# A Trainium2 decoder trunk: the front of the first feed-forward reordered, and more pairs of gate and up combined

## The chip, the cores and the metric

One core of a Trainium2 chip. The metric is the device time of one execution in microseconds; lower is better. A matrix product runs on TensorE (PE), elementwise work on VectorE (DVE), casts and activations on ScalarE (ACT), a few sums on GpSimd (POOL), and SyncE (SP) issues the transfers from main memory.

## The reference, cut to what matters

Two layers. Each has a feed-forward at half step, a mixing block (windowed attention beside gated linear attention), and a second feed-forward, so there are four feed-forwards, f = 0 to 3, on 512 tokens of width 1024:

```python
def rmsnorm(x, g):
    y = x * rsqrt(mean(x * x, axis=-1) + EPS)
    return y * g

def swiglu(h, w_gate, w_up, w_down):
    return (silu(h @ w_gate) * (h @ w_up)) @ w_down

h = rmsnorm(x, ffn1_norm[l])
x = x + 0.5 * swiglu(h, ffn1_w_gate[l], ffn1_w_up[l], ffn1_w_down[l])
```

w_gate and w_up are 1024 x 2816, w_down is 2816 x 1024. All inputs are float32.

## The kernel before, in words

x lies transposed: eight tiles x[d] of 128 features by 512 tokens. To keep float32 accuracy every operand of a large product is split into a rounded high half (a cast on ScalarE, line 112) and the rest (a subtraction on DVE, line 113), and each product is three matmuls, high by high, high by low, low by high (`mul3`, lines 182 to 184). Weights come as raw tiles of 1 MB in two buffers, issued on SP; their halves go into six rotating buffers each of `whi` and `wlo`, 512 columns apiece.

The 2816 hidden features are 22 blocks of 128, taken in two halves h of 11. For one block the columns of gate and up are worked on together, as a pair (the loop over j in `ffn`). After 11 pairs the products with w_down follow (eight outputs d, `Weights(wd[f, h, d], ...)`), which are added to x.

A pair is done in one of two ways. `plain(j)`: eight steps k, and in each three matmuls for gate and three for up, 128 x 128 by 128 x 512, so 48 matmuls of 512 columns. `combined(j)`: a scheme that makes the 2 x 2 blocks of weights and tokens out of seven products instead of eight; each product runs over four pairs of steps with three matmuls of 256 columns, 84 in all. It needs seven pieces of weights instead of four, four sums of raw weights on DVE (lines 166 to 173, class `Combined`), and sums of the outputs (lines 363 to 387). Its last two products are put off into the next pair (`rest`, `left`). The tuple `PLAIN` (line 48) names the pairs that are plain, counted over both halves: the first five, and 8, 11, 15 and 19.

The norm of a feed-forward is not ready when its first pair starts. The first three pairs of h = 0 run on x times the gain alone (`Norm.scaled`, lines 218 and 219: operands `uh`, `ul`), and their outputs are multiplied by the norm's factor afterwards (lines 342 and 343, in `gated`). The factor comes in steps. `squares` squares x[d] on ScalarE and sums on POOL (lines 260 to 264); in the first feed-forward the squares of d = 5 to 7 are kept apart (`direct`, line 256) and summed by PE. `scale` sums over features with matmuls of one column (line 275) and takes the power on POOL (line 280); `spread` brings the factor to all partitions with matmuls by the identity (line 286) and a copy on ScalarE (`rb`, line 289). `whole(d)` then makes the normalised x and splits it again into the same `uh`, `ul` (line 227 and `split`), for the pairs from j = 3 on; `combine(n)` makes the token sums that combined pairs need (lines 236 to 239 and two splits). In the code `scale` stands in pair 1 at step 2 and `spread` there at step 6, `whole(k)` in pair 2, `combine` in pairs 3 and 4.

The order of work: the program is written out by hand, a scheduler then sorts each engine's instructions by a priority that follows the order in the code; `tc.high_priority(offset)` moves a block ahead by so much, `PREP` = 400 for weights and `FIRST` = 5000 for the first pair's weights with the loads of x and their splits. Buffers of a name (`temp(2)` has four, PSUM pools `mm` and `sm` four each) make later users wait. Each engine runs its instructions strictly in the sorted order.

At the very start (lines 820 to 831): the load of the small vectors, the first pair's weights mixed with the loads of x, the constants `cst` (identity, ones, masks of attention, cosines, sines), the masks `mi` with a cast on DVE, and the squares.

Of the kernel before, what the change touches and what calls it, by code (L numbers as in the profile page):

```python
# [17 lines left out]
P = 128  # L18
# [3 lines left out]
KD = D // P  # L22
FF = 2816
NF = FF // P
NH = NF // 2
# [9 lines left out]
FIRST = 5000  # L35


C_ID, C_TRI, C_ONE, C_BO, C_AM, C_COS, C_SIN = 0, 128, 256, 257, 289, 545, 1057
# [6 lines left out]

H = T // 2

PLAIN = (0, 1, 2, 3, 4, 8, 11, 15, 19)

VB = 144  # L50
VCUT = (0, 400, 784, 1168)
# [3 lines left out]
def trunk(ctx, tc, xT, wgu, wd, wqk, wv, wg, wpa, wpb, wo, glaw, vecs, consts, masks, out):  # L55
    nc = tc.nc
    V, S, G, PE = nc.vector, nc.scalar, nc.gpsimd, nc.tensor
# [11 lines left out]
    def slot(tag, shape=(P, T), dtype=F32, bufs=1):  # L69
        big = int(np.prod(shape[1:])) >= 256  # L70
        return (pool if big else tiny).tile(list(shape), dtype, name=tag, tag=tag, bufs=bufs)

    def temp(n, shape=(P, T)):
        return slot(f"t{n}", shape, bufs=4)
# [4 lines left out]
    def psum():  # L79
        return sm.tile([P, T], F32, name="sm", tag="sm")  # L80

    def acc():
        return mm.tile([P, T], F32, name="mm", tag="mm")
# [7 lines left out]
    cst = cpool.tile([P, NCONST], F32, name="cst")  # L91
# [19 lines left out]
    def split(hi, lo, src):  # L111
        S.copy(hi, src)  # L112
        V.tensor_sub(lo, src, hi.bitcast(F32))  # L113
# [66 lines left out]
    def mul3(ps, w, a, start, stop, onto=False):  # L180

        PE.matmul(ps, w[0], a[0], start=start, stop=False, skip_group_check=onto)  # L182
        PE.matmul(ps, w[0], a[1], start=False, stop=False, skip_group_check=onto)  # L183
        PE.matmul(ps, w[1], a[0], start=False, stop=stop, skip_group_check=onto)  # L184
# [107 lines left out]
    def ffn(f, norm, nxt, spill, last):  # L292
        for h in range(2):
            g = []

            rest = []
            room = {}

            def left(n=2):
                while n and rest:  # L300
                    rest.pop(0)()
                    n -= 1

            def part(tag, n):

                if tag not in room:
                    room[tag] = slot(tag, (P, 2, T), F32R)
                return room[tag][:, n, :]

            def keep(j, tu):  # L310
                if j < 8:
                    hi, lo = slot(f"{'qk'[j % 2]}{j // 2}", dtype=F32R), part(f"v{j // 2}", j % 2)
                else:
                    hi, lo = (part(f"{sets[1]}{2 * z + (j - 8) // 2}", j % 2) for z in range(2))
                split(hi, lo, tu)
                g.append((hi, lo))

            def silu(to, z):
                tables[0] = S.activation(to, z, AF.Silu)

            def plain(j):
                raw = h == 0 and j < 3
                w = first if f + h + j == 0 else Weights(wgu[f, h * NH + j], KD, 256)
                pg, pu = acc(), acc()
                for k in range(KD):
                    if h == 0 and j == 1 and k == 2:
                        norm.scale()
                    if h == 0 and j == 1 and k == 6:
                        norm.spread()
                    if k in (2, 5):  # L330
                        left(1)
                    mul3(pg, w.at(k, 0, P), norm.u[k], k == 0, k == KD - 1)
                    mul3(pu, w.at(k, P, P), norm.u[k], k == 0, k == KD - 1)
                    if h == 0 and j == 2:
                        norm.whole(k)
                    if h == 0 and j in (3, 4) and k in (3, 7):
                        norm.combine(2 * j - 6 + k // 4)

                def gated():
                    tg, tu = temp(1), temp(2)  # L340
                    if raw:
                        V.tensor_mul(tg, pg, norm.rb)
                        V.tensor_mul(tu, pu, norm.rb)
                        silu(tg, tg)
                        V.tensor_mul(tu, tu, tg)
                    else:
                        silu(tg, pg)
                        V.tensor_mul(tu, pu, tg)
                    keep(j, tu)

                return gated

            def combined(j):
                w = Combined(wgu[f, h * NH + j])

                def run(to, n, start=False):
                    for k in range(4):
                        mul3(to, w.at(n, k), norm.c[k][n], start and k == 0, k == 3, not start)

                a = acc()[:, :H]  # L360
                run(a, 1, True)
                s12 = temp(1)
                S.copy(s12[:, :H], a)
                left(1)
                b = acc()[:, :H]
                run(b, 5, True)
                left(1)
                run(a, 6)
                S.copy(s12[:, H:], a)
                c = psum()[:, :H]  # L370
                run(c, 2, True)
                tg, su = temp(1), temp(2)
                V.tensor_add(tg[:, :H], c, s12[:, :H])
                run(a, 7)
                S.copy(su[:, :H], a)
                V.tensor_add(su[:, H:], b, su[:, :H])

                def up():
                    run(a, 4)

                def gate():
                    run(b, 3)
                    V.tensor_add(tg[:, H:], b, s12[:, H:])
                    silu(tg, tg)
                    tu = temp(2)
                    V.tensor_mul(tu[:, :H], a, tg[:, :H])
                    V.tensor_mul(tu[:, H:], su[:, H:], tg[:, H:])
                    keep(j, tu)

                rest.extend((up, gate))  # L390

            late = None
            for j in range(NH):
                if h * NH + j in PLAIN:
                    gated = plain(j)
                    if h == 0 and j == 0:
                        late = gated
                    else:
                        if late is not None:
                            late()  # L400
                            late = None
                        gated()
                else:
                    combined(j)
            left()
            for d in range(KD):
                w = Weights(wd[f, h, d], NH, P)
                ps = acc()
                for k in range(NH):
                    mul3(ps, w.at(k, 0, P), g[k], k == 0, k == NH - 1)  # L410
                V.scalar_tensor_tensor(x[d], ps, 0.5, x[d], op0=ALU.mult, op1=ALU.add)
                if h == 1:
                    if nxt is not None:
                        nxt.add(d)
                    if spill or last:
                        nc.sync.dma_start((xs if spill else out)[:, d, :], x[d])
# [400 lines left out]
    norm = Norm(0, V_F1)  # L817
# [3 lines left out]

    with tc.high_priority(offset=FIRST):
        nc.scalar.dma_start(vec, vecs)
    first = Weights(wgu[0, 0], KD, 256, 2, FIRST, (load, norm.scaled))
    mi = slot("v0", (P, 576), I32)
    with tc.high_priority(offset=PREP):
        nc.sync.dma_start(cst, consts)
        nc.sync.dma_start(mi, masks)
    for d in range(KD):
        norm.squares(d, d > 4)  # L830
    V.tensor_copy(msk, mi)

    ones = temp(1)
# [4 lines left out]
    for l in range(L):  # L838
        n2 = Norm(l, V_MIX)
        ffn(2 * l, norm, n2, True, False)  # L840
        g = temp(1)[0:96]
        nc.scalar.dma_start(g, glaw[:, l, :])
        n3 = Norm(l, V_F2)
        mix(l, n2, n3, g)
        norm = Norm(l + 1, V_F1) if l + 1 < L else None
        ffn(2 * l + 1, n3, norm, False, l + 1 == L)
# [117 lines left out]
```

## Time and profile before

| | us |
|---|---|
| median of three runs | 2351.91 (2349.49 to 2353.78) |
| the profiled execution | 2350.56 |
| its span on the core | 2348.8 |
| TensorE busy | 2323.8 (99%) |
| VectorE busy | 1520.7 (65%) |
| ScalarE busy | 1114.4 (47%) |
| POOL busy | 154.1 (7%) |

The page's busy times are averages over stages that differ; where work follows work its rows have a start and a duration. Operations of one engine overlap in part, so the distance from start to start says what one costs in a row, and the duration says when its result is there. A group of rows shows an idle time with its releaser in square brackets.

### The profile page before, as it was taken

How to read it: one execution, taken by the hardware profiler on the slowest of the kernel's cores; microseconds unless marked ns; L12 is line 12 of the kernel's file. 1: busy time of each engine (PE TensorE's matmuls, PEld its weight loads, DVE VectorE, ACT ScalarE, POOL GpSimd, SP SyncE). 2: the span in 40 equal slices, each digit the busy share in tenths (PEclk: the TensorE clock that was granted, in tenths of full speed). 3: DMA queues.
4: the chain of work that ended last, by engine and by line, in shares of the span. 5: the costliest groups of instructions: out<-in, count | busy, mean ns of one | idle time of the engine just before them, and what ended most of it. 6: DMA issues, size and time to landing. Idle time of an engine off the chain costs nothing.

```text
span 2348.8 us, 33948 instructions
## 1 busy us (share of the span) xinstructions
PE 2323.8 (99%) x12904; PEld 2011.7 (86%) x12904; DVE 1520.7 (65%) x2769; ACT 1114.4 (47%) x2077; POOL 154.1 (7%) x147
## 2 busy tenths in 40 slices
PE   8999999999999999999999999999999999999999
PEld 7889988787888889899889899887878888898997
DVE  7846755659755678467468467456596556773772
ACT  5534544554455345245445345454545644552551
POOL 1000010003110100000100000100131101000000
PEclk9999999999999999999999999999999999999999
DMA  5232234121123322322322322431112233223232
GB/s 179 75 111 97 101 122 135 64 81 37 55 90 117 117 90 85 122 91 96 111 90 85 122 90 87 144 123 64 68 37 72 90 125 109 90 92 115 90 100 90
DMA packets 73587, 226.68 MB, mean 97 GB/s; under 512 B 8720, under 2 KB 16912, under 8 KB 73424
## 3 DMA queue, kind: packets, MB, share of 16 engines
q1 hardware_dynamic: 71136, 221.46, 27.6%
q10 hardware_dynamic: 2288, 3.06, 0.5%
q8 instruction: 101, 1.65, 0.3%
q14 instruction: 62, 0.51, 0.1%
HBM read 215.58 MB, written 6.29 MB: 94 GB/s over the span
## 4 chain that ended last, share of the span: by engine, by line
PE 90%; DVE 7%; ACT 2%; issue 1%; POOL 0%; DMA 0%; SPq 0%; DVEq 0%; POOLq 0%; ACTq 0%
PE mm L182 26%; PE mm L184 26%; PE mm L183 25%; PE sm L674 2%; DVE wlo L113 1%; PE mm L518 1%; PE mm L520 1%; PE mm L519 1%; PE sm L183 1%; PE sm L182 1%; PE sm L184 1%; PE sm L580 1%; PE sm L611 1%; PE sm L605 1%; DVE t L658 0%
## 5 line engine op out<-in xcount | busy, mean ns | idle before, releaser
L112 ACT CAST whi<-raw 128x512 fp32r<-128x512 f32 (+2 forms) x976 | 588.9, 608 | 917.8 <-PE mm L183 798.6
L113 DVE TENSOR_TENSOR wlo<-raw,whi 128x512 fp32r<-128x512 f32 (+2 forms) x976 | 669.3, 690 | 491.5 <-ACT whi L112 480.3
L182 PE MATMUL mm<-uh,whi 128*128 128x512 f32 (+1 forms) x1584 | 579.7, 366 | 6.5 <-ACT uh L218 5.7
L183 PE MATMUL mm<-ul,whi 128*128 128x512 f32 (+1 forms) x1584 | 577.6, 365 | 0.0
L184 PE MATMUL mm<-uh,wlo 128*128 128x512 f32 (+1 forms) x1584 | 575.6, 364 | 1.0 <-DVE wlo L113 0.9
L182 PEld LDWEIGHTS mm<-uh,whi 128*128 128x128 f32 x1584 | 300.3, 190 | 52.0 <-ACT uh L218 5.7
L184 PEld LDWEIGHTS mm<-uh,wlo 128*128 128x128 f32 x1584 | 299.9, 189 | 49.0 <-DVE wlo L113 4.0
L183 PEld LDWEIGHTS mm<-ul,whi 128*128 128x128 f32 x1584 | 300.5, 190 | 44.7 <-DVE ul L219 0.5
L183 PE MATMUL mm<-v,whi 128*128 128x512 f32 x640 | 249.1, 389 | 0.0
L183 PEld LDWEIGHTS mm<-v,whi 128*128 128x128 f32 x640 | 120.2, 188 | 24.3
L182 PE MATMUL mm<-k,whi 128*128 128x512 f32 x320 | 124.6, 389 | 0.0
L182 PE MATMUL mm<-q,whi 128*128 128x512 f32 x320 | 124.5, 389 | 0.0
L184 PE MATMUL mm<-k,wlo 128*128 128x512 f32 x320 | 124.5, 389 | 0.0
L184 PE MATMUL mm<-q,wlo 128*128 128x512 f32 x320 | 124.5, 389 | 0.0
L264 POOL TENSOR_TENSOR sum<-sum,t 128x512 f32<-128x512 f32 x39 | 53.5, 1372 | 681.0 <-ACT t L263 385.3
L182 PE MATMUL mm<-b,whi 128*128 128x256 f32 (+1 forms) x272 | 85.9, 317 | 0.1
L184 PE MATMUL mm<-qr,wlo 128*128 128x256 f32 (+1 forms) x272 | 83.7, 308 | 0.0
L182 PE MATMUL mm<-qr,whi 128*128 128x256 f32 (+1 forms) x272 | 83.7, 308 | 0.0
L184 PE MATMUL mm<-b,wlo 128*128 128x256 f32 (+1 forms) x272 | 83.7, 308 | 0.0
L183 PE MATMUL mm<-o,whi 128*128 128x512 f32 x192 | 75.2, 392 | 0.0
L183 PE MATMUL mm<-x,whi 128*128 128x512 f32 x192 | 75.2, 392 | 0.0
L182 PEld LDWEIGHTS mm<-k,whi 128*128 128x128 f32 x320 | 60.1, 188 | 12.6
(326 smaller groups left out, 4218.6 us busy)
## 6 DMA issues: line engine op xcount, KB each, us to landing
raw<-in_wgu SPq DMA_DIRECT2D x174, 512.0 KB, 4.1
raw<-in_wd SPq DMA_DIRECT2D x64, 512.0 KB, 3.6
raw<-in_wg SPq DMA_DIRECT2D x48, 512.0 KB, 4.4
raw<-in_wqk SPq DMA_DIRECT2D x26, 512.0 KB, 4.4
raw<-in_wd SPq DMA_DIRECT2D x64, 192.0 KB, 3.7
raw<-in_wpb SPq DMA_DIRECT2D x16, 512.0 KB, 4.2
raw<-in_wo SPq DMA_DIRECT2D x16, 512.0 KB, 5.8
raw<-in_wv SPq DMA_DIRECT2D x16, 384.0 KB, 3.3
```

Source lines behind the costliest of these rows:

```text
L112: S.copy(hi, src)
L113: V.tensor_sub(lo, src, hi.bitcast(F32))
L182: PE.matmul(ps, w[0], a[0], start=start, stop=False, skip_group_check=onto)
L183: PE.matmul(ps, w[0], a[1], start=False, stop=False, skip_group_check=onto)
L184: PE.matmul(ps, w[1], a[0], start=False, stop=stop, skip_group_check=onto)
L264: G.tensor_tensor(self.sum, self.sum, sq, op=ALU.add)
L518: PE.matmul(ps, u[k][0][:, t], wh, start=k == 0, stop=False)
L519: PE.matmul(ps, u[k][0][:, t], wl, start=False, stop=False)
L520: PE.matmul(ps, u[k][1][:, t], wh, start=False, stop=k == KD - 1)
L580: PE.matmul(ps[half][:, j, k0:], stacked[2 * jp + j][:, half, t], z[:, half, n * P - P + k0:(n + 1) * P], start=z is kh, stop=z is kl)
L605: row = after(PE.transpose(pt[:, kc, j, :], s[half][:, j, kc * P:(kc + 1) * P], ident), row)
L674: PE.matmul(ps[:, i, :], ke[:, i, :], qe[:, i * 64:(i + 1) * 64], start=True, stop=True)
```

## The change

PLAIN keeps the first five pairs; 8, 11, 15 and 19 are combined. In the first feed-forward pair 5 is plain as well. There the second pair's weights get a higher priority, the sums of squares all go over POOL, `scale`, `spread`, `whole` and `combine` come later in the code, the gating of pairs 0 and 1 is put off until the factor is spread, pair 2 takes its accumulators from the other PSUM pool, five matmuls on zeros are put at the very start, and the constants are loaded in two parts, of which only the first keeps a priority, with the masks behind the second.

```diff
-PLAIN = (0, 1, 2, 3, 4, 8, 11, 15, 19)
+PLAIN = (0, 1, 2, 3, 4)
+
+COMBINE = (((3, 7), (4, 3), (4, 7), (5, 3)), ((3, 3), (3, 7), (4, 3), (4, 7)))
...
             def plain(j):
                 raw = h == 0 and j < 3
-                w = first if f + h + j == 0 else Weights(wgu[f, h * NH + j], KD, 256)
-                pg, pu = acc(), acc()
+                w = (first, second)[j] if f + h == 0 and j < 2 else Weights(wgu[f, h * NH + j], KD, 256)
+                pg, pu = (psum(), psum()) if f + h == 0 and j == 2 else (acc(), acc())
                 for k in range(KD):
-                    if h == 0 and j == 1 and k == 2:
+                    if h == 0 and (j, k) == ((1, 2) if f else (1, 6)):
                         norm.scale()
-                    if h == 0 and j == 1 and k == 6:
+                    if h == 0 and (j, k) == ((1, 6) if f else (2, 2)):
                         norm.spread()
+                        while late and not f:
+                            late.pop(0)()
...
-                    if h == 0 and j == 2:
-                        norm.whole(k)
-                    if h == 0 and j in (3, 4) and k in (3, 7):
-                        norm.combine(2 * j - 6 + k // 4)
+                    if h == 0 and j == 2 and (f or k > 1):
+                        for d in range(0 if k == 2 and not f else k, k + 1):
+                            norm.whole(d)
+                    if h == 0 and (j, k) in COMBINE[f > 0]:
+                        norm.combine(COMBINE[f > 0].index((j, k)))
...
-            late = None
+            late = []
             for j in range(NH):
-                if h * NH + j in PLAIN:
+                if h * NH + j in PLAIN or f + h == 0 and j == 5:
                     gated = plain(j)
-                    if h == 0 and j == 0:
-                        late = gated
-                    else:
-                        if late is not None:
-                            late()
-                            late = None
-                        gated()
+                    late.append(gated)
+                    while late and not (h == 0 and j < (1 if f else 2)):
+                        late.pop(0)()
...
     with tc.high_priority(offset=FIRST):
         nc.scalar.dma_start(vec, vecs)
+
+        z, ps = temp(2), psum()
+        V.memset(z, 0.0)
+        for _ in range(5):
+            PE.matmul(ps[:, :H], z[:, :P], z[:, :H], start=True, stop=True)
     first = Weights(wgu[0, 0], KD, 256, 2, FIRST, (load, norm.scaled))
+    second = Weights(wgu[0, 1], KD, 256, ahead=FIRST // 2)
     mi = slot("v0", (P, 576), I32)
     with tc.high_priority(offset=PREP):
-        nc.sync.dma_start(cst, consts)
-        nc.sync.dma_start(mi, masks)
+        nc.sync.dma_start(cst[:, :C_BO], consts[:, :C_BO])
+    nc.sync.dma_start(cst[:, C_BO:], consts[:, C_BO:])
+    nc.sync.dma_start(mi, masks)
     for d in range(KD):
-        norm.squares(d, d > 4)
+        norm.squares(d)
     V.tensor_copy(msk, mi)
```

## Rows read from the trace of the kernel before

**Rows 1.** The head of the page, and its chain of work that ended last.

```profile
span 2348.8 us, 33948 instructions
...
PE 2323.8 (99%) x12904; PEld 2011.7 (86%) x12904; DVE 1520.7 (65%) x2769; ACT 1114.4 (47%) x2077; POOL 154.1 (7%) x147
...
PE 90%; DVE 7%; ACT 2%; issue 1%; POOL 0%; DMA 0%; SPq 0%; DVEq 0%; POOLq 0%; ACTq 0%
```

**Rows 2.** Timeline of PE, 0 to 70 us: start, duration, operation, idle before.

```profile
5.65 0.79 PE L182 MATMUL mm<-uh,whi 128*128 128x512 f32 x1 [5.65 <-ACT uh L218]
...
8.31 0.63 PE L184 MATMUL mm<-uh,wlo 128*128 128x512 f32 x1
...
18.20 0.39 PE L184 MATMUL mm<-uh,wlo 128*128 128x512 f32 x1
19.40 0.50 PE L182 MATMUL mm<-uh,whi 128*128 128x512 f32 x1 [0.82 <-ACT whi L112]
...
22.63 0.72 PE L275 MATMUL sm<-cst,t 128*128 128x1 f32 x6
...
26.19 0.77 PE L182 MATMUL mm<-uh,whi 128*128 128x512 f32 x1
...
33.30 1.05 PE L286 MATMUL sm<-cst,rstd 128*128 128x128 f32 x8
...
36.94 0.39 PE L182 MATMUL mm<-uh,whi 128*128 128x512 f32 x1
...
69.58 0.28 PE L182 MATMUL mm<-uh,whi 128*128 128x256 f32 x1
```

**Rows 3.** Stretches: length, busy by engine, granted clock, DMA share, GB/s.

```profile
26.00:28.00 2.00, 2.00 (x7) 1.66 (x7) 0.77 (x2) 0.00 (x0) 1.39 (x1) 0.51 0.22 86
28.00:30.00 2.00, 2.00 (x7) 1.58 (x6) 0.00 (x0) 0.00 (x0) 0.02 (x1) 0.63 0.00 0
```

**Rows 4.** Timelines of DVE, POOL and ACT, 13 to 19 us.

```profile
13.18 1.48 DVE L113 TENSOR_TENSOR wlo<-raw,whi 128x512 fp32r<-128x512 f32 x1 [0.23 <-ACT whi L112]
...
15.24 1.78 DVE L219 SCALAR_TENSOR_TENSOR ul<-x,vec,uh 128x512 fp32r<-128x512 f32 x1
...
15.05 4.57 POOL L264 TENSOR_TENSOR sum<-sum,t 128x512 f32<-128x512 f32 x3 [0.95 <-ACT t L263]
...
18.21 0.63 ACT L256 ACTIVATE t<-x 128x512 f32<-128x512 f32 x1 [1.07 <-POOL sum L264]
```

**Rows 5.** The factor and the last normalised x; stretches (PE, PEld, DVE, ACT, POOL).

```profile
34.39 0.59 ACT L289 COPY rb<-sm 128x512 f32<-128x512 f32 x1 [0.50 <-PE sm L286]
...
55.05 0.68 DVE L113 TENSOR_TENSOR ul<-o,uh 128x512 fp32r<-128x512 f32 x1
...
34.50:85.00 50.50, 50.20 (x273) 43.32 (x272) 49.24 (x89) 30.33 (x53) 0.00 (x0) 1.00 0.21 74
85.00:116.00 31.00, 30.77 (x208) 28.02 (x208) 24.03 (x44) 16.69 (x32) 0.00 (x0) 1.00 0.28 101
```

**Rows 6.** A run of combined pairs: PE at its two ends, and its stretch.

```profile
245.69 0.28 PE L182 MATMUL mm<-uh,whi 128*128 128x256 f32 x1
...
273.04 0.40 PE L182 MATMUL mm<-uh,whi 128*128 128x512 f32 x1
...
245.70:273.00 27.30, 27.30 (x229) 27.30 (x228) 23.43 (x42) 16.92 (x33) 0.00 (x0) 1.00 0.33 116
```

**Rows 7.** Timeline of DVE within combined pairs, one operation behind another.

```profile
218.81 0.42 DVE L386 TENSOR_TENSOR t<-mm,t 128x256 f32<-128x256 f32 x1
219.14 0.68 DVE L168 TENSOR_TENSOR raw<-raw 128x512 f32<-128x512 f32 x1
219.74 0.68 DVE L113 TENSOR_TENSOR wlo<-raw,whi 128x512 fp32r<-128x512 f32 x1
```

**Rows 8.** Timeline of PE: a later feed-forward's sums, and f32 matmuls in the mixing.

```profile
839.50 0.94 PE L275 MATMUL sm<-cst,sum 128*128 128x1 f32 x8
...
595.07 1.03 PE L720 MATMUL sm<-v,attn 128*128 128x256 f32 x4
```

## The prediction

> **What bounds the kernel now.** I read the head of the page first: of a span of 2348.8 us TensorE (PE) is busy for 99%, and the chain that ended last is PE for 90% [rows 1]. So time is won only by giving PE less to do, or by closing the few places where it runs slowly or waits. The PE timeline of the first 70 us shows those places [rows 2]; the table of stretches gives the clock granted there [rows 3]; the rows of the other engines show what feeds PE in the front [rows 4] and how full VectorE (DVE) is behind it [rows 5]. Then come a run of combined pairs on PE [rows 6] and on DVE [rows 7], and two prices of operations that the change uses [rows 8].
>
> The reader is to see three things. A plain pair of gate and up costs 48 matmuls of 512 columns, a combined one 84 of 256. The front loses some 9 us of PE to slow or empty stretches, once per kernel. And DVE, not PE, is full from 35 to 85 us [rows 5]: there the first feed-forward rests on DVE's order of work.
>
> A change is told from none here at about 0.2%, 4.7 us.
>
> **The pairs.** From 36.94 to 69.58 PE ran three plain pairs, 144 matmuls [rows 2]: 0.2267 each, so 10.88 us a pair. From 245.69 to 273.04 it ran 228 matmuls of combined pairs [rows 6]: 0.1200 each, so 84 of them take 10.08. A pair saved is 0.80 us; a plain pair between combined ones also loses a little at each switch, which I allow up to 0.1 for. The feed-forwards with f = 1 to 3 turn four pairs each (8, 11, 15, 19), f = 0 the same four but takes pair 5 back: 3 + 12 = 15 pairs. 15 x 0.80 = 12.0; with the switches 13.5 at most; I take **12.7**.
>
> The half-width pitch is not half of the full one: the two rows fit a fixed 13 ns per matmul plus 0.417 ns a column. Combining pays while 36 more matmuls cost less than 3072 fewer columns, so up to a fixed part of 36 ns. The Trainium skill (TensorE: Matmul & The Clock Gate, section Back-to-back issue gap) speaks against the change: it gives a sustained 81 ns for 128 columns and 131 ns for 512, between which 256 would lie near 98, an estimate of mine. By that a combined pair would take 8.2 us and a plain one 6.3, and 15 pairs would lose 29 us. The trace disagrees with both levels (120 and 227 ns), and the sum goes by the trace.
>
> **What the combined pairs ask of DVE.** A plain pair in this stage needs six operations of 512 columns there (four low halves of weights, a product, a low half kept), a combined one twelve of 512 (seven low halves, four sums of raw weights, one kept) and five of 256. Back to back they start 0.60 and 0.33 us apart [rows 7]: 12 x 0.60 + 5 x 0.33 = 8.9 us, under the 10.08 of PE. The run of nearly three combined pairs shows DVE at 23.43 of 27.30 us, with PE busy throughout [rows 6]; ScalarE, with seven casts a pair, is at 16.92, and a pair's DMA is the same 1 MB as before. So longer runs, eleven in the second half, should hold: cost nothing, covered by DVE's 10%. Where that cover is thin is the first half: DVE is full until 85 and has 31.0 - 24.03 = 7.0 us free from 85 to 116 [rows 5]. With pair 8 combined it does 8.9 - 3.6 = 5.3 us more, and PE takes 0.8 us less: 0.9 us of slack is left over three pairs. I charge f = 1 to 3 with 0.5 us each, **1.5** (from 0, if the order falls well, to 4.5, three times the 1.5 us that a late weight or two would cost). In f = 0 pair 5, now plain, takes the same 5.3 us off DVE, so nothing is charged.
>
> **The front, once per kernel.** Each step is counted on PE.
>
> The dummy matmuls. The real ones start slowly, five in the 2.66 us from 5.65 to 8.31 [rows 2], 0.53 each against 0.2267 later. That is the pace of the stretch from 26 to 30, where the granted clock is 0.51 and 0.63 on the mean, 1.2 GHz for most of it and 2.4 at its end [rows 3]; ahead of 5.65 PE had done nothing, ahead of 26 only one-column matmuls. Five of 256 columns in f32, of which two take 1.03 us at 2.4 GHz [rows 8], last at most 5.2 us at 1.2 GHz and fit roughly ahead of 5.65, when the first operand arrives. They may push the first matmul back by up to 1 us. But the end of pair 0 is set by supply: the last low half of x ends at 15.24 + 1.78 = 17.02 [rows 4], five matmuls follow, 18.2 against 18.4 before. The faster clock is worth only **0.2**; 1.2 if that low half comes sooner, -0.5 if more POOL sums hold it back.
>
> The second pair's weights, raised over squares, constants and masks. Before, PE went idle at 18.4, ran from 19.40 and came to the sums of squares at 22.63: 4.2 us for 12 matmuls worth 2.7 [rows 2]. ScalarE was in the squares then, one of which waited 1.07 us for POOL [rows 4]. With weights ahead of constants on SP's queue and ahead of squares on ScalarE, most of 1.5 comes back: **1.4** (0.7 to 1.5).
>
> The squares, all summed on POOL. 32 instructions took 22.63 to 26.19, 3.56 us [rows 2]; eight, as in the other feed-forwards, take 0.94 at most [rows 8]: **2.7** saved. PE's clock then stays up: 24 matmuls took 7.11 us up to 33.30 and would take 5.44: **1.7**. The price is three more POOL additions: three took 4.57 us [rows 4], so seven end near 15.05 + 6 x 1.52 = 24.2 if squares come in time, and PE asks at 26.4. They also hold DVE up: operations beside them took 1.48 and 1.78 us [rows 4] where alone they take some 0.7 [rows 7]. One DVE operation per addition still gives a low half each 1.5 us, where PE takes one per 2.72.
>
> The sum so far is 0.2 + 1.4 + 2.7 + 1.7 = 6.0: pair 3 would start at 41.8 and not at 47.8 (36.94 + 10.88).
>
> What is late next. The spread factor is on ScalarE until 34.98 [rows 5]; after, the spread sits at step 2 of pair 2, 32.8, and the factor is there at about 34.3: hardly earlier, with PE 6 us on. From it DVE must do the gated parts of pairs 0 and 1 (8 operations), 16 for the normalised x and some 6 low halves: 30 x 0.62 = 18.6, so the last x at 52.9. PE wants it at 41.8 + 7 x 1.36 = 51.3. Before it came 20.8 us behind the factor (55.05 + 0.68 less 34.98), which would be 55.1. The wait is 0 to 3.8; I take **2.0**. Pair 2 takes its two accumulators from the other PSUM pool, since the four of the first stay taken until the gating of pairs 0 and 1; pair 3 has them back after four products on DVE, ahead of its x. On SP's queue pair 1's two loads pass the constants and masks; the slice with ones and identity goes right behind them, long before 26, and the rest is read in the mixing only. The cast of the masks follows its DMA and falls ahead of the factor, where DVE is not yet full. All of that I cost at nothing.
>
> Front: 6.0 - 2.0 = **4.0** (1.5 to 6.5).
>
> **Sum.** 12.7 - 1.5 + 4.0 = 15.2 below the profiled execution's 2350.56, which is 2348.8 of span and 1.8 around it: 2335.4. The median of the three runs lies 1.35 higher, so I say **2336**.
>
> **Rivals.** (a) The front gives nothing: PE's lead turns wholly into waits for the normalised x. For it: DVE was busy 49.24 of 50.50 us there, and its factor comes hardly earlier. Against: pair 5, plain, relieves it. 2351.9 - 11.2 = 2340.7. (b) DVE becomes the bound of the long runs. If operations took their full durations, 12 x 0.68 + 5 x 0.42 = 10.3 us a pair, it would just exceed PE's; over 67 combined pairs (17 in three feed-forwards, 16 in the first) it decides from (16.7 + 4.7) / 67 + 10.08 = 10.4 on. At 10.7, with one round trip of 0.3 to ScalarE unhidden in each, 67 x 0.6 = 40 lost, 2375. Against: the starts are 0.60 apart, and DVE idles in the run. (c) The fixed cost per matmul is over 36 ns where combined pairs follow each other for long: at 60 ns a pair would lose 36 x 0.060 - 3072 x 0.000417 = 0.88 us, 15 of them 13, 2361 with the front's gain. The run at 120 ns speaks against it, for it is such a run. The figures quoted above from TensorE: Matmul & The Clock Gate in the Trainium skill are of this kind. (d) Late weights in f = 1 to 3 take back what their 12 pairs save, and the front gives nothing: three pairs are left, 2351.9 - 2.5 = 2349, no change.
>
> **How the numbers follow.** Forecast 0.70, (a) 0.18, (b) 0.03, (c) 0.01, (d) 0.08. Ends: 13.5 + 6.5 = 20.0 gives 2332, rounded out to 2330; 12.0 - 4.5 + 1.5 = 9.0 gives 2343, and 2345 takes in most of (a) and none of (b) to (d). Faster is the forecast and (a): 0.88; same (d), 0.08; slower (b) and (c), 0.04.
>
> **What would show it.** Of after: no 512-column matmuls between combined pairs in the second half, and runs of eleven at 0.12 us; DVE under full there. Pair 1 starts at the heels of pair 0; eight small matmuls, and a granted clock of 1.0 behind them. Pair 3 waits about 2 us for `ul` or `uh`. The prediction is wrong if PE waits for `wlo` in the long runs, if the sum on POOL ends after PE asks for it, or if the wait for the normalised x is near 0 or 6.

## The result, and the profile of the changed kernel

The changed kernel takes 2338.07 us in the median of four runs (2336.97 to 2339.81), the kernel before, run beside it, 2351.93 (2349.49 to 2353.78): a ratio of 0.9941, with a 95% interval of 0.9929 to 0.9953. It is faster by 13.9 us; 2336 was forecast, within 2330 to 2345. The profiled execution took 2339.81 us, with a span of 2338.0, so the two profiles lie 10.8 us apart.

The head of the page after answers to [rows 1]: TensorE (PE) runs 526 instructions more in 7.8 us less, VectorE (DVE) is at 68%.

```profile
span 2338.0 us, 35293 instructions
...
PE 2316.0 (99%) x13430; PEld 2030.5 (87%) x13430; DVE 1592.8 (68%) x2935; ACT 1156.7 (49%) x2167; POOL 159.3 (7%) x150
```

To see where the 10.8 us lie I cut both executions at the matmuls that sum the squares: one row of them begins each feed-forward from f = 1 on, and each mixing block. Here are their rows in the timeline of PE after, and then those of before (the second of before, at 839.50, is in [rows 8]).

```profile
362.98 0.95 PE L277 MATMUL sm<-cst,sum 128*128 128x1 f32 x8
...
831.85 0.95 PE L277 MATMUL sm<-cst,sum 128*128 128x1 f32 x8
...
1183.78 0.95 PE L277 MATMUL sm<-cst,sum 128*128 128x1 f32 x8
...
1526.84 0.94 PE L277 MATMUL sm<-cst,sum 128*128 128x1 f32 x8
...
1995.97 0.95 PE L277 MATMUL sm<-cst,sum 128*128 128x1 f32 x8
```

```profile
372.35 0.94 PE L275 MATMUL sm<-cst,sum 128*128 128x1 f32 x8
...
1193.32 0.94 PE L275 MATMUL sm<-cst,sum 128*128 128x1 f32 x8
...
1538.77 0.95 PE L275 MATMUL sm<-cst,sum 128*128 128x1 f32 x8
...
2004.71 0.95 PE L275 MATMUL sm<-cst,sum 128*128 128x1 f32 x8
```

The differences of neighbouring starts, and of the last start to the end of the span, give the length of each part (us):

| part | before | after | after less before | forecast |
|---|---|---|---|---|
| first feed-forward, with the front | 372.35 | 362.98 | -9.37 | -6.5 |
| mixing 1 | 467.15 | 468.87 | +1.72 | 0 |
| f = 1 | 353.82 | 351.93 | -1.89 | -2.9 |
| f = 2 | 345.45 | 343.06 | -2.39 | -2.9 |
| mixing 2 | 465.94 | 469.13 | +3.19 | 0 |
| f = 3, to the end | 344.09 | 342.03 | -2.06 | -2.9 |

(The forecast column is the prediction's: 4.0 for the front and 12.7 / 15 = 0.85 a pair, three pairs in the first feed-forward, four in each other, less 0.5 there.) The sum came out near partly by luck, since its misses partly cancel: the first feed-forward gave 2.9 more than forecast, the others 2.4 less, and the mixing, which the change doesn't touch, took 4.9.

**The front.** The timeline of PE after, to hold against [rows 2]:

```profile
1.45 4.52 PE L829 MATMUL sm<-t 128*128 128x256 f32 x10 [1.45 <-DVE t L827]
...
17.96 0.39 PE L184 MATMUL mm<-uh,whi 128*128 128x512 f32 x1
...
26.21 0.94 PE L277 MATMUL sm<-cst,sum 128*128 128x1 f32 x8
...
33.70 1.16 PE L288 MATMUL sm<-cst,rstd 128*128 128x128 f32 x8 [0.94 <-POOL rstd L282]
...
42.89 0.39 PE L184 MATMUL mm<-uh,whi 128*128 128x512 f32 x1
...
55.16 0.47 PE L185 MATMUL mm<-ul,whi 128*128 128x512 f32 x1
...
75.89 0.28 PE L184 MATMUL mm<-uh,whi 128*128 128x256 f32 x1
```

The 49th matmul of 512 columns, the first of pair 1, begins at 17.96 without a wait (18.2 was forecast), the eight sums come at 26.21 (26.4), pair 3 begins at 42.89 (41.8), and the clock stays up behind them, as the stretches say (length, busy by engine, granted clock, DMA share, GB/s), where [rows 3] had 0.51 and 0.63. The last row is the long run of combined pairs in the second half of this feed-forward:

```profile
26.00:28.00 2.00, 2.00 (x14) 1.81 (x13) 0.93 (x2) 0.62 (x1) 0.00 (x0) 1.00 0.69 249
28.00:30.00 2.00, 2.00 (x10) 1.62 (x9) 0.00 (x0) 0.15 (x1) 0.00 (x0) 1.00 0.68 214
...
186.78:294.77 107.99, 107.99 (x902) 107.99 (x900) 96.40 (x176) 66.31 (x127) 0.99 (x2) 1.00 0.30 103
```

Then PE waits 0.94 us for the factor, from POOL. The timelines of SP, DVE and POOL show why it is late:

```profile
24.65 0.43 SPq L836 DMA_DIRECT2D v<-in_masks  x1
...
13.46 3.16 DVE L221 SCALAR_TENSOR_TENSOR ul<-x,vec,uh 128x512 fp32r<-128x512 f32 x2 [0.26 <-ACT uh L220]
...
31.64 0.46 DVE L839 CAST msk<-v 128x576 uint8<-128x576 int32 x1 [4.70 <-DMA v<-in_masks]
32.01 0.15 DVE L280 TENSOR_SCALAR ms<-sm 128x4 f32<-128x4 f32 x1
...
14.71 9.87 POOL L266 TENSOR_TENSOR sum<-sum,t 128x512 f32<-128x512 f32 x6 [0.34 <-ACT t L265]
32.25 1.40 POOL L282 TENSOR_TENSOR rstd<-ms,mhalf 128x4 f32<-128x4 f32 x1 [7.67 <-DVE ms L280]
```

POOL's sum ends at 14.71 + 9.87 = 24.58 (24.2 forecast), in time. But the masks' load, now behind other weights on SP, is issued at 24.65, and DVE stands 4.70 us in front of their cast, with `ms` queued behind it; POOL has waited 7.67 us for `ms`.

**The first half of f = 1.** The stretch of the plain pairs before, then after, and that of the combined pairs behind them after:

```profile
846.70:882.18 35.48, 35.48 (x160) 29.37 (x159) 35.04 (x62) 21.25 (x35) 0.00 (x0) 1.00 0.22 77
...
839.05:874.53 35.48, 35.48 (x160) 29.37 (x158) 34.97 (x62) 21.27 (x35) 0.00 (x0) 1.00 0.23 78
874.53:935.68 61.15, 60.31 (x481) 58.30 (x480) 55.00 (x104) 37.18 (x73) 0.00 (x0) 1.00 0.28 94
```

DVE has no room beside the plain pairs (34.97 of 35.48), and the 480 matmuls of 256 columns that follow take 61.15 us, 0.1274 each; at the 0.1200 of [rows 6] they would take 57.6. The lost 3.5 us are spread over pairs 5 to 8: PE's waits there end at low halves of the token sums (`ga`, `ke`) and of weights (`wlo`) and at sums of outputs (`t`), nearly all made by DVE. The timeline of PE gives pair 5's first matmul and the first of the last pair's put-off products, before and then after (pair 5 starts at 874.53 after):

```profile
882.18 0.28 PE L182 MATMUL mm<-uh,whi 128*128 128x256 f32 x1
...
944.26 0.39 PE L182 MATMUL mm<-b,whi 128*128 128x256 f32 x1
```

```profile
936.75 0.39 PE L184 MATMUL mm<-b,whi 128*128 128x256 f32 x1
```

From the one to the other it is 62.1 us before and 62.2 after, although pair 8 is combined after.

### The profile page after: what moved, and what is told of

Its sections match the earlier page's. It is cut to its first block, busy times and chain, and to the rows that moved or that the text cites. A ratio compares the mean times of both kernels' runs of the same rounds, so it can differ in the third digit from the quotient of the medians.

```text
span 2338.0 us, 35293 instructions
## 1 busy us (share of the span) xinstructions
PE 2316.0 (99%) x13430; PEld 2030.5 (87%) x13430; DVE 1592.8 (68%) x2935; ACT 1156.7 (49%) x2167; POOL 159.3 (7%) x150
## 3 DMA queue, kind: packets, MB, share of 16 engines
q8 instruction: 105, 1.72, 0.3%
## 4 chain that ended last, share of the span: by engine, by line
PE 88%; DVE 7%; ACT 2%; DMA 2%; issue 1%; POOL 0%; SPq 0%; DVEq 0%; POOLq 0%; ACTq 0%
PE mm L184 25%; PE mm L185 25%; PE mm L186 25%; PE sm L675 2%; DVE wlo L115 1%; PE sm L184 1%; PE sm L185 1%; PE sm L186 1%; PE mm L519 1%; DMA raw<-in_wgu 1%; PE mm L521 1%; PE mm L520 1%; PE sm L581 1%; PE sm L612 1%; PE sm L606 1%
## 5 line engine op out<-in xcount | busy, mean ns | idle before, releaser
L114 ACT CAST whi<-raw 128x512 fp32r<-128x512 f32 (+1 forms) x1021 | 618.1, 609 | 899.8 <-PE mm L185 746.7
L115 DVE TENSOR_TENSOR wlo<-raw,whi 128x512 fp32r<-128x512 f32 (+1 forms) x1021 | 704.4, 693 | 440.0 <-ACT whi L114 429.9
L184 PE MATMUL mm<-uh,whi 128*128 128x512 f32 (+1 forms) x1448 | 512.3, 355 | 0.9 <-DVE t L388 0.6
L185 PE MATMUL mm<-ul,whi 128*128 128x512 f32 (+1 forms) x1448 | 511.6, 353 | 0.1
L186 PE MATMUL mm<-uh,wlo 128*128 128x512 f32 (+1 forms) x1448 | 508.6, 352 | 0.7 <-DVE wlo L115 0.7
L184 PEld LDWEIGHTS mm<-uh,whi 128*128 128x128 f32 x1448 | 274.4, 190 | 38.9 <-DVE t L381 1.6
L185 PEld LDWEIGHTS mm<-ul,whi 128*128 128x128 f32 x1448 | 275.0, 190 | 36.7 <-DVE ul L221 1.5
L184 PE MATMUL sm<-uh,whi 128*128 128x256 f32 (+1 forms) x284 | 82.2, 289 | 0.0
L185 PE MATMUL sm<-ul,whi 128*128 128x256 f32 (+1 forms) x284 | 82.0, 289 | 0.0
L186 PE MATMUL sm<-uh,wlo 128*128 128x256 f32 (+1 forms) x284 | 82.0, 289 | 0.0
```

## The experiments

Each short diff is against the changed kernel unless another is named. First the two parts of the change alone.

**pairs_only** is the kernel before with the tuple alone:

```diff
-PLAIN = (0, 1, 2, 3, 4, 8, 11, 15, 19)
+PLAIN = (0, 1, 2, 3, 4)
```

> The old front with only the first five pairs of every feed-forward plain, so 16 pairs are newly combined. Theory A (VectorE is the limit in the first halves): combining pair 8 there brings nothing, and each of the three pairs in a second half brings about 0.68 us, so each feed-forward gains about 2.0 us, the first one too, 8 in all; the other three stay where they stand in the changed kernel (343 to 352 us from one sum of squares to the next). Theory B (TensorE alone decides, 0.8 us a pair): 12.8 us in all, 3.2 in each. The mixing may differ by some us either way with the clock granted in it.

Measured: 2345.01 us, ratio 0.9968 [0.9958, 0.9979]. f = 1 to 3 took 351.83, 344.05 and 341.76 us: 2.0, 1.4 and 2.3 less than before, much as in the changed kernel (1.9, 2.4 and 2.1), so their gain is the pairs'. The first feed-forward took 371.5, 0.85 less, where 2.0 was expected. But its front, that of before unchanged, had a worse start in the profiled execution: the low clock lasted from 5.98 to 11.97, where in the profile of before it ended at 9.09, and again longer behind the squares, so the spread came at 34.91 and not at 33.30. Without these 1.6 us, if all of them reach the end, it would have gained 2.5.

**front_only** keeps the rest of the change and pairs 8, 11, 15 and 19 plain:

```diff
-PLAIN = (0, 1, 2, 3, 4)
+PLAIN = (0, 1, 2, 3, 4, 8, 11, 15, 19)
```

> The new front with pairs 8, 11, 15 and 19 plain again (and pair 5 of the first feed-forward plain). If the front and the pairs are separate, the first feed-forward ends 2.0 to 2.8 us later than in the changed kernel, so near 365.5 us and 7 us ahead of the kernel before (372.35), and the later feed-forwards are as before; in all 6 to 7 us faster than before. If the front's gain needs the combined pairs behind it, or was an accident of the clock, it is under 4.

Measured: 2349.15 us, ratio 0.9988 [0.9979, 0.9997], 3.3 us less than the kernel before beside it, where 6 to 7 were expected. The first feed-forward took 367.28, 5.07 less than before, the other three as before (353.85, 345.46, 344.36). Its spread came at 34.64, 0.94 later than the changed kernel's. The two parts alone make 0.85 + 5.07 = 5.9 us in the first feed-forward, and 8.5 with the 1.6 and 0.94 us by which their fronts were slower; together they make 9.37. Within a microsecond they add up, and one front differs by about as much between executions (the sums come at 26.21 in the changed kernel and at 27.05 here). In the medians the parts make 7.4 and 3.3 us, 10.7 together, against 13.9 for the whole; the intervals do not tell that from a plain sum.

Next the front, step by step.

**masks_early** loads the masks ahead of the rest of the constants:

```diff
         nc.sync.dma_start(cst[:, :C_BO], consts[:, :C_BO])
+        nc.sync.dma_start(mi, masks)
     nc.sync.dma_start(cst[:, C_BO:], consts[:, C_BO:])
-    nc.sync.dma_start(mi, masks)
```

> The changed kernel with the masks loaded right behind the first slice of constants, as early as before. Theory: VectorE stood 4.7 us at the cast of the masks, and behind it stood the small operation for the norm's factor; with the masks there early this wait goes, the factor is ready some 4 us sooner, TensorE does not wait 0.94 us for it, and the normalised x comes earlier: the first feed-forward 1.0 to 1.6 us shorter, 361.4 to 362.0 us. Rival: TensorE is held by VectorE's amount of work until about 80 us and the wait is only moved: 0 to 0.2 us.

Measured: 2338.13 us, ratio 0.9942 [0.9927, 0.9956], the time of the changed kernel. The timelines of DVE and PE show the wait gone, and a later one:

```profile
23.35 1.55 DVE L839 CAST msk<-v 128x576 uint8<-128x576 int32 x1
...
32.60 1.05 PE L288 MATMUL sm<-cst,rstd 128*128 128x128 f32 x8
...
235.16 0.69 DVE L168 TENSOR_TENSOR raw<-raw 128x512 f32<-128x512 f32 x1 [0.77 <-DMA raw<-in_wgu]
...
237.78 0.38 PE L184 MATMUL mm<-uh,whi 128*128 128x256 f32 x1 [0.39 <-DVE t L381]
```

Pair 6 started at 74.71 and not at 75.89, 1.18 us sooner, and the long run of the second half at 185.39 and not at 186.78, 1.39 sooner; at the next sum of squares 0.74 was left (362.24). The rest went in that run, whose 900 matmuls took 108.64 us for 107.99: PE waits at 237.78 for DVE's sum `t`, and DVE had stood 0.77 us at 235.16, in front of a sum of raw weights whose load was late, with `t` queued behind it. The cause of the 0.94 us is shown; as a saving it is under what the medians tell apart.

**loads_as_before** takes all three load edits back:

```diff
-    second = Weights(wgu[0, 1], KD, 256, ahead=FIRST // 2)
+    second = Weights(wgu[0, 1], KD, 256)
...
-        nc.sync.dma_start(cst[:, :C_BO], consts[:, :C_BO])
-    nc.sync.dma_start(cst[:, C_BO:], consts[:, C_BO:])
-    nc.sync.dma_start(mi, masks)
+        nc.sync.dma_start(cst, consts)
+        nc.sync.dma_start(mi, masks)
```

> The changed kernel with both edits on loads undone: the second pair's weights at the usual priority, constants and masks ahead of them. Theory: what removed the wait between pairs 0 and 1 was that 1.07 MB of constants and masks no longer go ahead of the second pair's weights; with them back, TensorE waits there 1.0 to 1.5 us again and comes to the sums of squares at 27 to 27.5 and not at 26.2. Rival: the rearranged squares removed it, and it stays at 26.2 or less.

Measured, in a single execution: 2336.19 us; sums at 26.41, no wait between pairs 0 and 1, the spread at 32.80 without a wait, first feed-forward 361.76, 1.22 less than in the changed kernel. So the wait between pairs 0 and 1, at 19.40 in [rows 2], stays away without the weights' higher priority: the rest of the change is enough. What differs on ScalarE is the order of its casts: the first high half of pair 1's weights came at 18.75 before, behind all the squares, and comes at 15.16 here, ahead of four of them.

**second_late** takes back the first of these lines alone:

> The changed kernel with the second pair's weights at the priority of all other weights. Theory: TensorE waits for them between pair 0 and pair 1, as before, 1.0 to 1.5 us, and the first feed-forward is as much longer. Rival: ScalarE is free enough by then, and it is 0 to 0.4.

Measured, in a single execution: 2335.7 us, sums at 25.86, no wait between the pairs, first feed-forward 361.92. It agrees: the raised weights were not needed for that, and the wait of 1.0 to 1.5 us did not come back. In this execution the masks' cast came at 28.67 and not at 31.64, and the factor was not waited for, so raising the weights also helped to make the masks late. (Squares_direct, below, has no wait between the pairs either, its pair 1 beginning at 17.94, but it keeps the raised weights. No run takes back both the loads and the squares, so it is open whether either is enough or another edit, as the later place of `scale` in the code, did it.)

**no_warm** cuts the five dummies to one matmul of one column:

```diff
-        for _ in range(5):
-            PE.matmul(ps[:, :H], z[:, :P], z[:, :H], start=True, stop=True)
+        PE.matmul(ps[:, :1], z[:, :P], z[:, :1], start=True, stop=True)
```

> The changed kernel with the five matmuls on zeros cut down to one of a single column. Theory of the forecast: the last low half of x sets the end of pair 0, so the faster start is worth only 0.2 us (0 to 0.5): pair 1's sums still begin near 26.3, the first feed-forward ends near 363.2. Rival: the whole slow stretch at the start is on the path, 1.5 to 3 us (six to thirteen matmuls at 0.43 and not 0.23).

Measured, in a single execution: 2337.52 us. The timeline of PE shows the slow start back, matmuls of 512 columns 0.42 apart at 7.33:

```profile
7.33 0.63 PE L186 MATMUL mm<-uh,wlo 128*128 128x512 f32 x1
7.75 0.63 PE L184 MATMUL mm<-uh,whi 128*128 128x512 f32 x1
```

The sums came at 26.93, 0.72 later; but the factor was then waited for no longer (spread at 33.32), and the first feed-forward took 362.60, 0.38 less. The dummies bring at most 0.7 us as far as the sums, which is no more than executions differ (front_only, with the dummies, came to them at 27.05), and nothing at the end.

**squares_direct** sums the squares of d = 5 to 7 on PE again:

```diff
-        norm.squares(d)
+        norm.squares(d, d > 4)
```

> The changed kernel with the squares of d = 5 to 7 kept apart and summed by TensorE again, 32 one-column instructions for 8. Theory: 2.7 us more on TensorE for them, and 1.7 us or more behind them because the clock falls again: the first feed-forward 4.4 us longer (3.5 to 5.5), less what the wait of 0.94 for the factor hides. Rival: only part of it counts, since VectorE holds TensorE until 80 us: under 2.5.

Measured, in a single execution: 2340.96 us. The block of one-column matmuls lasted from 26.22 to 30.00, and the stretches behind it have the low clock back:

```profile
30.00:32.00 2.00, 2.00 (x6) 1.61 (x7) 0.77 (x2) 0.00 (x0) 1.41 (x1) 0.50 0.03 12
32.00:34.00 2.00, 2.00 (x9) 1.58 (x8) 0.00 (x0) 0.00 (x0) 0.00 (x0) 0.80 0.00 0
```

The spread came 36.89 - 33.70 = 3.2 us later, and the first feed-forward took 2.84 more. The terms of 2.7 and 1.7 add to 4.4; 2.97 us for the block (3.78 against 0.81) and 1.3 for the clock were found, 4.3 together, of which the 0.94 us of the masks' wait hides a part.

Last the pairs.

**pair5_plain** makes pair 5 plain in all four feed-forwards:

```diff
-                if h * NH + j in PLAIN or f + h == 0 and j == 5:
+                if h * NH + j in PLAIN or h == 0 and j == 5:
```

> The changed kernel with pair 5 plain in all four feed-forwards, not in the first alone: three pairs fewer are combined. Theory A (VectorE limits the first halves of f = 1 to 3): the waits around the first combined pairs there, some 3.5 us in each, mostly go, as they are nearly absent in the first feed-forward; against 0.8 us more of matmuls this gives 2.0 to 2.4 us less in each, 6 to 7 in all. Theory B (TensorE's matmuls decide): three pairs at 0.8 us, 2.4 us more.

Measured: 2331.5 us (2329.03 to 2334.24), ratio 0.9917 [0.9901, 0.9934], faster than the changed kernel (each of its four executions is under each of the other's). f = 1 to 3 took 350.15, 341.43 and 339.29 us, 6.2 less together, though a plain pair costs PE 0.8 more. The stretches of the first half of f = 1 are:

```profile
836.34:882.70 46.36, 46.36 (x207) 38.38 (x206) 43.54 (x78) 27.15 (x45) 0.00 (x0) 1.00 0.24 82
882.70:930.21 47.51, 47.51 (x397) 47.51 (x396) 41.68 (x75) 29.29 (x57) 0.00 (x0) 1.00 0.29 98
```

Now DVE has some room in the plain stretch, and the combined pairs behind it run at 47.51 / 396 = 0.1200. The first halves alone, from the sum of squares to the put-off products, became 2.5 to 2.6 us shorter in each; the long runs of the second halves took 0.9 back in f = 1 and again in f = 2.

**first5_combined** goes the other way, with pair 5 of the first feed-forward combined too (its token sums then come a little sooner):

```diff
-COMBINE = (((3, 7), (4, 3), (4, 7), (5, 3)), ((3, 3), (3, 7), (4, 3), (4, 7)))
+COMBINE = (((3, 7), (4, 3), (4, 5), (4, 7)), ((3, 3), (3, 7), (4, 3), (4, 7)))
...
-                if h * NH + j in PLAIN or f + h == 0 and j == 5:
+                if h * NH + j in PLAIN:
```

> The changed kernel with pair 5 of the first feed-forward combined, as in the others, and the token sums made earlier in the code to suit. Theory A (VectorE limits): the first feed-forward is 2 us longer (1.5 to 4), with waits of TensorE at the first combined pairs. Theory B (TensorE's matmuls decide): 0.8 us shorter.

Measured, in a single execution: 2350.37 us. The first feed-forward took 373.74, 10.8 us more than in the changed kernel, where 1.5 to 4 were expected, and more than before. In the timeline of PE the first combined pair waits for operands made by ACT and DVE, and in the stretches PE is half empty beside a full DVE and the clock falls as well:

```profile
73.13 0.50 PE L184 MATMUL mm<-ga,whi 128*128 128x256 f32 x2 [1.11 <-ACT ga L114]
...
77.54 0.79 PE L184 MATMUL mm<-attn,whi 128*128 128x256 f32 x2 [1.51 <-ACT attn L114]
```

```profile
70.00:75.00 5.00, 2.52 (x18) 2.04 (x16) 4.99 (x10) 1.78 (x4) 0.00 (x0) 1.00 0.45 156
75.00:80.00 5.00, 3.20 (x15) 3.00 (x16) 4.58 (x10) 1.74 (x3) 0.00 (x0) 0.72 0.00 0
```

The faster front alone, then, runs into DVE's backlog and gives all of its gain back; pair 5, plain, lets it through. It does so in two ways that no run separates: it asks less of DVE, and it puts off by a pair the time at which the token sums (`ga`, `attn` in the rows) must be there.

**both** joins masks_early and pair5_plain.

> Masks early and pair 5 plain in all four feed-forwards together. If the two are separate, 2331.5 less 0.5 to 1.2, so near 2330.6 us; the first feed-forward near 362, the others 350.2, 341.4, 339.3. If VectorE's work in the first half hides the earlier factor, no difference from 2331.5.

Measured: 2331.61 us (2327.94 to 2335.67), ratio 0.9912 [0.9899, 0.9926]: no different from pair5_plain.

**best** joins pair5_plain and loads_as_before.

> The changed kernel with pair 5 plain in all four feed-forwards, and the second pair's weights, the constants and the masks loaded as in the kernel before. Theory: the two savings lie at different places and add up. The first feed-forward takes about 361.8 us from sum of squares to sum of squares (362.98 in the changed kernel, 361.76 with the loads as before), the others 350.2, 341.4 and 339.3 as with pair 5 plain; the median lies about 1.2 us under that kernel's, near 2330.3. Rival: what is won ahead of pair 3 is given back later in the first feed-forward, to DVE, as with the early masks: the first feed-forward stays at 362.5 or more and the median at 2331.5, no change from pair 5 plain alone. The stretches of the mixing are 465.9 to 469.1 each under both.

Measured: 2331.32 us (2327.02 to 2332.66), ratio 0.9902 [0.9885, 0.9918]. The first feed-forward took 362.75, so the rival's number came, but not by its path. The second half's long run began at 185.77, 1.01 us ahead of the changed kernel; its 900 matmuls took 108.76 us, where the same code in loads_as_before took 108.00 and kept the lead. As with the early masks DVE stood there, 0.65 us at 235.66, for a late load of weights. In f = 2 of this execution that cost most, 110.32 us for the 900, and the timelines of DVE and PE show it:

```profile
1435.15 0.69 DVE L168 TENSOR_TENSOR raw<-raw 128x512 f32<-128x512 f32 x1 [1.97 <-DMA raw<-in_wgu]
...
1437.77 0.39 PE L184 MATMUL mm<-uh,whi 128*128 128x256 f32 x1 [1.62 <-DVE t L381]
```

The three kernels with pair 5 plain cannot be told apart; all are some 6.5 us faster than the changed one and 20.9 to 22.1 faster than the kernel before beside them.

**The mixing.** Its instructions are the same before and after, yet it took 4.9 us more. Mixings differ from one another in one place, behind a wait of 2.3 us in which PE stands for DVE. The timeline of PE after, in the first mixing, has

```profile
523.43 0.65 PE L671 MATMUL sm<-t,ke 128*64 128x64 f32 x8 [2.34 <-DVE t L666]
```

Ten microseconds that begin within 0.8 us ahead of that row, in both mixings, have in the stretches of after, and then of before, a granted clock under 1.00 in three places of four (1.00 is 2.4 GHz, 0.50 is 1.2):

```profile
522.98:532.98 10.00, 9.55 (x45) 8.47 (x46) 6.34 (x15) 2.92 (x5) 3.45 (x4) 0.66 0.00 1
1686.84:1696.84 10.00, 9.29 (x44) 8.34 (x45) 6.34 (x16) 2.92 (x5) 3.45 (x4) 0.66 0.00 0
```

```profile
532.35:542.35 10.00, 9.67 (x57) 8.63 (x58) 7.94 (x18) 2.81 (x5) 3.45 (x4) 0.83 0.03 7
1698.77:1708.77 10.00, 9.69 (x62) 8.22 (x63) 9.35 (x22) 3.57 (x7) 3.46 (x4) 1.00 0.14 45
```

Over the 26 mixings of the thirteen profiles that leave this place as it is (before, after and all runs but fill), the granted clock there is 1.00 in five, 0.83 in seven and 0.66 in fourteen, and the whole mixing takes 465.9 to 466.3, 467.2 to 467.5 and 468.6 to 469.1 us, without an overlap. Two of 0.66 after against 0.83 and 1.00 before make the 4.9 us. As the same kernel shows different values at its two mixings (1.00 and 0.66 in best), it is no fixed property of the change.

**fill** tries to end the fall, on top of both: once in each mixing, five f32 matmuls of 256 columns, whose result nobody uses, are chained in front of the matmuls that wait. The edit also ties those matmuls into one order, and in every head of the linear attention, not in the first alone.

```diff
+                    fill = None
+                    if h == 0:
+                        spare = psum()
+                        for _ in range(5):
+                            fill = after(PE.matmul(spare[:, :256], ident, dec[:, 0, :], start=True, stop=True), fill)
...
-                        PE.matmul(ps[0:w, i, :], ke[:, i, 0:w], qe[:, i * w:(i + 1) * w], start=True, stop=True)
+                        fill = after(PE.matmul(ps[0:w, i, :], ke[:, i, 0:w], qe[:, i * w:(i + 1) * w], start=True, stop=True), fill)
```

> The kernel of the run before with five f32 matmuls of 256 columns put into each mixing, where TensorE waits 2.3 us for VectorE ahead of the first products of the linear attention; their result is not used. Theory: the granted clock falls behind that wait, in some executions for 3 us, in some for 6, and costs the 1.6 or 3.2 us by which the mixings differ between the profiles (466, 467.2, 468.9 us); with the wait filled the clock stays at 1.00 and both mixings take 466 to 466.5, so 1.5 to 2.5 us less in the median and less spread. Rival: the fall has another cause, as the many matmuls of 64 columns behind the wait: the granted clock and the spread stay, and the time is the same or up to 2 us more.

Measured: 2345.51 us, ratio 0.9973 [0.9964, 0.9982], 13.9 us slower than both. Neither the theory nor its rival had foreseen that. The first wait shrank to 0.56 us, but the chain brought new waits for DVE, and behind them the clock fell all the same; the mixings took 476.0 and 476.5 us. The timeline of PE and the stretches show it:

```profile
522.46 0.65 PE L676 MATMUL sm<-t,ke 128*64 128x64 f32 x8 [0.56 <-DVE t L666]
...
527.27 1.08 PE L680 MATMUL sm<-t,ke 128*128 128x64 f32 x8 [1.68 <-DVE t L666]
...
601.38 1.97 PE L680 MATMUL sm<-t,ke 128*128 128x64 f32 x8 [3.56 <-DVE x L763]
```

```profile
522.01:532.01 10.00, 7.88 (x48) 7.01 (x49) 8.31 (x18) 3.45 (x6) 3.91 (x4) 0.83 0.00 1
...
600.00:611.00 11.00, 9.62 (x41) 9.23 (x42) 5.23 (x11) 3.63 (x7) 2.54 (x3) 0.53 0.18 66
```

As each fall here still came in or behind a wait, of 1.68 and of 3.56 us, the run does not show whether the wait is the cause. Nor can the wait alone explain the three values, since it lasted 2.31 to 2.37 us in all 26 mixings. What decides between them stays open.

## Why the prediction was right, and where not

**The pairs, 0.80 to 0.9 each (12.7).** Right where they run in the second halves. The 900 combined matmuls there take 107.99 us in the first feed-forward, 0.1200 each, and 108.48, 108.21 and 108.34 in f = 1 to 3. The three pairs of a second half gave 2.52 us (0.84 each) in the first feed-forward and 2.04 (0.68) in f = 1. Rivals (b) and (c) fall with this: DVE is at 96.40 of 107.99 us in such a run. But PE is not free of waits there, as the prediction had it: in f = 1 it waits once for DVE's `t`, behind a late load of weights, and with pair 5 plain such waits cost up to 2.3 us in a run (best, 110.32). So DVE's 10% cover its amount of work, and not a load that comes late. (a) falls with the 9.37 us of the first feed-forward; (d), late weights, is right in kind but small. By the Trainium skill (TensorE: Matmul & The Clock Gate, section Back-to-back issue gap), with its 131 ns for 512 columns and the estimate of 98 for 256 made from it, combined pairs would have lost; the trace disagrees, at 227 and 120.

**DVE in the first halves, 1.5 in all.** The place was right, the term mis-sized. Pair 8 combined gave nothing: from pair 5's start to the put-off products of the first half f = 1 took 62.2 us where it took 62.1 before, and f = 2 and 3 are alike (62.0 and 62.2 for 62.1). Its own gain of 0.8 went, so the charge is 0.7 to 0.9 a feed-forward, not 0.5, and about 2.5 for the three rather than 1.5. The prediction took the slack that pair 8 uses from the row of the first feed-forward, 7.0 us in 31 [rows 5], and so missed that DVE enters this stretch late: it had been full beside the plain pairs, 35.04 of 35.48 us in f = 1 before.

**Pair 5 plain, charged and credited with nothing but its pair.** This was the step that missed most. From the start of pair 5 to the put-off products of the first half the changed kernel took 59.8 us in the first feed-forward and the kernel before 62.1, 2.3 less, although pair 5 is plain there. In pair5_plain the same edit gave 1.8, 1.6 and 2.7 us in f = 1 to 3, and without it (first5_combined) the front's gain is lost, 10.8 us. The prediction saw DVE full from 35 to 85 us and then priced its relief at zero, as if a wait that isn't there could not be removed; but the kernel before had lost 2.3 us there, 216 matmuls in 28.19 us in place of 25.9.

**The front, 4.0.** The size was right, in part by luck: two of its parts miss in opposite directions. Pair 5 starts at 75.89 - 10.88 = 65.01 where it started at 69.58 [rows 2]: 4.57. Of the four gains, the squares (2.7) and the clock behind them (1.7) are borne out by squares_direct, at 3.0 and 1.3. The weights' higher priority (1.4) was credited with what the other edits do without it: the wait did go, but it stays away when the priority is taken back. The dummies' 0.2 is 0.7 at most to the sums, within what executions differ, and nothing at the end. The wait for the normalised x (2.0) did not come, though its two ends were read rightly: the last low half of x is there at 54.40 + 0.68 = 55.08 (54.9 to 55.1 forecast), and PE takes one at 55.16. But 53 matmuls stand ahead of that one from the first of pair 3 on, more than the 48 of a pair, so the scheduled order had put matmuls of pair 4 ahead of it; the step that failed took PE to go through pair 3 in the order of the code. From pair 3 to pair 5 only 0.4 us were lost: the lead is 47.82 - 42.89 = 4.9 at the one and 4.57 at the other. By the prediction's own sign, a wait near 0, this term was wrong. What came instead was earlier: PE waited 0.94 us for the factor, because of the masks' cast, **which the prediction had costed at nothing**: it placed the cast "ahead of the factor, where DVE is not yet full". A full DVE was not the question. The cast's data was late, behind another weight's load on SP, and DVE, which works strictly in order, stood 4.70 us in front of it.

**The mixing, no change.** Not in the sum, and worth 4.9 us in these two profiles, along with a clock that differs from one execution to the next.

The near hit is thus 2.9 us too little for the first feed-forward, 2.4 too much for the others and 4.9 unforeseen: 15.2 + 2.9 - 2.4 - 4.9 = 10.8.

## What to carry to other kernels

A feeder that is full for a whole stretch leaves a debt which the next stretch pays: a pair that costs the fed engine 0.8 us more there, but asks less of the feeder and gives it more time, won 1.6 to 2.7 us net. Where an edit sets back a load, look for the instruction that reads it on an engine working in order, and at what stands behind that instruction: here it was the masks' cast once, and sums of raw weights now and then. And cut two profiles into the same parts before judging an edit: a part that the edit doesn't touch moved by 4.9 us, against 10.8 in all.

## What had not been expected of the hardware

The granted clock behind one and the same 2.3 us wait of PE takes three mean values, 1.00, 0.83 and 0.66 over ten microseconds, worth 0, about 1.3 and about 2.7 us, and one execution can show two of them. The slow start of the kernel varies too: the same front ended it at 9.09 us before and at 11.97 in pairs_only. The Trainium skill (TensorE: Matmul & The Clock Gate, section What's actually happening) says of a kernel's start that the number of slow matmuls differs from run to run of one kernel. The trace agrees, and shows the like in the midst of a kernel.

Operations of DVE beside POOL's additions took 3.16 / 2 = 1.58 us for a low half that takes some 0.7 alone, and the masks' cast 1.55 us beside them (masks_early) against 0.46 without. The additions themselves took 9.87 / 6 = 1.65 us each.
